# Every fourth low part of the weights: an accumulating DMA onto -hi in place of a subtraction on VectorE

## The chip, the cores and the metric

The kernel runs on one core of one Trainium2 chip. The metric is device time in microseconds (us) of one execution; lower is better. The engines are called as the profile calls them: PE (TensorE, matrix products), DVE (VectorE), ACT (ScalarE), POOL (GpSimd) and SP (SyncE, which issues most DMAs). hi and lo are the two parts of a number, explained below.

## What is computed

One decoder block over 256 tokens of width 2048 in float32, with two attention branches, gates and a feed-forward part. Cut to its products:

```python
xn = rmsnorm(h, attn_norm)
q_a, k_a, v_a, c_q, c_kv, k_r, gates = split(xn @ w_in)
y_a = moba_attention(rope(q_a), rope(k_a), v_a)              # 8 heads of 128
qh = rmsnorm(c_q, q_norm) @ w_uq;  kv = rmsnorm(c_kv, kv_norm) @ w_ukv
y_b = mla_attention(q_nope, rope(q_rope), k_nope, rope(k_r), v_b)
mixed = g_a * (y_a @ w_branch_a) + g_b * (y_b @ w_branch_b)
h = h + mixed @ w_out
hn = rmsnorm(h, ffn_norm)
h = h + (silu(hn @ w_gate) * (hn @ w_up)) @ w_down           # d_ff = 5632
out = rmsnorm(h, final_norm)
```

Both attentions are causal over the 256 tokens. Most of the work is the products with the large weights (about 62 million numbers, each read once).

## The kernel before

Each matrix product is made of float32r passes. An operand is cut into hi (its rounding to float32r) and lo = operand - hi, and hi*hi + lo*hi + hi*lo is summed in PSUM. The activations are stationary (128 rows of the contraction by 128 tokens, two token tiles); the weights stream past them in slabs of 128 rows by 512 columns.

A list of products (`job`) is cut into groups of up to four slabs and into steps of two slabs. There are 468 steps of weights. From the first gate product of the feed-forward part on (`ga0`, step 204) they are 11 pairs of products with w_gate and w_up (176 steps) and 4 products with w_down (88 steps). The last six steps run for one token tile and then for the other.

Work that surrounds one step s:

- `load(g)` (line 722) issues on SP the DMA of one group of weights, 128 x 4 x 512 numbers (1024 KB), into one of four raw tiles. It is called from `split` at the last step of a group, for the group four further on, and has to wait until that raw tile has been read.
- `split(s)` (line 731) makes the pair of weight tiles `wh`, `wl` (two slabs, 128 x 1024 numbers, 512 KB each) from the raw tile: ACT casts hi (line 742), DVE subtracts (line 743). The pool `splitp` has four buffers of each kind (AHEAD + 1), and `split` runs three steps ahead of the products (line 792).
- The products of step s (lines 802 to 810): for each of the two slabs and two token tiles a matmul of wh with the activation's hi, then of wh with its lo (line 805), then of wl with hi (line 810). Twelve matmuls in all. Between the steps stand the small works of attention, transposes and norms, put there by `later` and `at`.

So the wh buffer of step s is free after the eighth matmul of the step, the wl buffer after the twelfth, and both are next used by step s + 4. Every engine works through its instructions in order. The order is the one in which the program issues them (a manual schedule); waits between engines are semaphores. POOL has only a handful of fills at the start.

The lines that the change touches:

```python
nc.scalar.copy(hi, v)
nc.vector.tensor_sub(lo, v, f32(hi))
splits[s] = (hi, lo)
if st["end"]:
    del raws[st["g"]]
    load(st["g"] + RAWS)
```

Of the kernel before, what the change touches and what calls it, by code (L numbers as in the profile page):

```python
"""Hybrid decoder block (MoBA + MLA branches, sigmoid gates, SwiGLU FFN) on one core.

Every matrix product runs in float32r passes: an operand is cut exactly into hi (the float32r
rounding of it) and lo = operand - hi, and hi*hi + lo*hi + hi*lo is summed in float32 in PSUM.
Activations are stationary (transposed, [K, tokens]); weights stream through as [K, 512] slabs.
RMSNorm: gains are applied per partition while the transposed operand leaves PSUM, the
1/rms per token while the product leaves PSUM.
"""
# [2 lines left out]

# [11 lines left out]
OP = mybir.AluOpType  # L23

P = 128
NT = 2
S = NT * P
# [15 lines left out]
START = 8  # L43
# [19 lines left out]
def block_kernel(ctx: ExitStack, tc, x, positions, attn_norm, w_in, q_norm, w_uq, kv_norm, w_ukv,  # L63
                 w_branch_a, w_branch_b, w_out, ffn_norm, w_gate, w_up, w_down, final_norm,
                 inv_freq, out):
    nc = tc.nc
# [8 lines left out]
    def const(shape, name, dt=F32):  # L75
        return consts.tile(shape, dt, name=name)

    def big(shape, name, dt=F32):
        assert int(np.prod(shape[1:])) == 1024
        return tpool.tile(shape, dt, name=name, tag="T")  # L80

    def tps(shape, name):
        return psum.tile(shape, F32, name=name, tag="tp")

    f32 = lambda ap: ap.bitcast(F32)

    # ------------------------------------------------------------------ setup
    grow = [big([P, 1024], f"grow{i}")[:, :P] for i in range(2)]
    for g in grow:
        nc.vector.memset(g, 0.0)  # L90
# [19 lines left out]

    load_gain("attn", attn_norm)

    # mask: [tri | 0 | tri], added to scores [q, k]
    mask = const([P, 3, P], "mask")
    nc.gpsimd.memset(mask, 0.0)
    for j in (0, 2):
# [12 lines left out]
    def gain(key, k):  # L129
        return gT[key != "attn"][:, gcol[key] + k: gcol[key] + k + 1]  # L130

    # ------------------------------------------------------------ small helpers
    def rstd(ss, n, name):
        """ss [P, NT, m] partial sums of squares over n elements -> [P, NT] of 1/rms, in two parts."""
        v, r, t = [const([P, NT], name + x) for x in ("_v", "", "_t")]

        def root():
            nc.vector.tensor_reduce(out=v, in_=ss, axis=mybir.AxisListType.X, op=OP.add)
            nc.vector.tensor_scalar(v, v, 1.0 / n, EPS, op0=OP.mult, op1=OP.add)
            nc.scalar.activation(t, v, AF.Sqrt)  # L140

        def invert():
            nc.vector.reciprocal(r, t)
            nc.vector.tensor_mul(t, r, r)
            nc.vector.tensor_mul(t, t, v)
            nc.vector.tensor_scalar(t, t, -0.5, 1.5, op0=OP.mult, op1=OP.add)
            nc.vector.tensor_mul(r, r, t)
        return r, root, invert
# [4 lines left out]
        nc.scalar.activation(junk[:, :src.shape[-1]], src, AF.Square, accum_out=acc)  # L153

    def split_out(src, hi, lo, scale=None):
        """src -> hi + lo (float32r), scale a [P, 1] factor per partition."""
        if scale is None:
            nc.scalar.copy(hi, src)
            nc.vector.tensor_sub(lo, src, f32(hi))
        else:  # L160
            nc.scalar.mul(hi, src, scale)
            nc.vector.scalar_tensor_tensor(lo, src, scale, f32(hi), op0=OP.mult, op1=OP.subtract)

    def transpose4(nat, hi, lo, name, key=None, k0=0, nk=4, j0=0, first=False):
        """columns j0*128 .. nk*128 of nat [P tok, NT, :] -> hi, lo [P, :, S] at the same j, times the gains."""
        for j in range(j0, nk, 2):
            tp = tps([P, 2, S], f"{name}_tp{j}")
            for k in range(2):
                for t in range(NT):
                    nc.tensor.transpose(tp[:, k, t * P:(t + 1) * P],  # L170
                                        nat[:, t, (j + k) * P:(j + k + 1) * P], ident)
            if key is None:
                split_out(tp, hi[:, j:j + 2, :], lo[:, j:j + 2, :])
            else:
                gk = [gain(key, k0 + j + k) for k in range(2)]
                for k in range(2):
                    if first:
                        nc.vector.tensor_scalar(hi[:, j + k, :], tp[:, k, :], gk[k], None, op0=OP.mult)
                    else:
                        nc.scalar.mul(hi[:, j + k, :], tp[:, k, :], gk[k])  # L180
                for k in range(2):
                    nc.vector.scalar_tensor_tensor(lo[:, j + k, :], tp[:, k, :], gk[k], f32(hi[:, j + k, :]),
                                                   op0=OP.mult, op1=OP.subtract)
# [11 lines left out]
        nc.vector.tensor_sub(o1, ts[0], ts[1])  # L195
        nc.vector.tensor_add(o2, ts[2], ts[3])

    # ------------------------------------------------------------ rope tables
    rt = {}

    def rope_tables():
        """The parts, to be issued in this order. Angle / 2pi is summed from exact products of
        12-bit parts of the angle and of 1 / 2pi, whole turns taken off each."""
        v = nc.vector
        sh = [P, NT, 32]
        c = _inv2pi_parts()
# [1 line left out]
        a, ah, al = const(sh, "ang"), const(sh, "angh", F32R), const(sh, "angl")  # L208
# [50 lines left out]

        return [angles, products, sums, wrap, fold, sines]  # L260

    # ------------------------------------------------------------ streams
    jobs = []

    def job(w, kt, lhs, done, name):
        jobs.append(dict(w=w, kt=kt, n=w.shape[1], lhs=lhs, done=done, name=name))
# [8 lines left out]
        return lambda kt, t: (tiles_hi[kt // 4][:, kt % 4, t * P:(t + 1) * P],  # L275
                              tiles_lo[kt // 4][:, kt % 4, t * P:(t + 1) * P])

    # ------------------------------------------------------------ phase 1: x -> xT, projections
    ssx = const([P, NT, 4], "ssx")
    xh = [big([P, 4, S], f"xh{c}", F32R) for c in range(4)]  # L280
    xl = [big([P, 4, S], f"xl{c}", F32R) for c in range(4)]
# [20 lines left out]
    L = {}  # L302

    R["x"], x_root, x_invert = rstd(ssx, D, "rstd_x")
    ssq, sskv = const([P, NT, 1], "ss_q"), const([P, NT, 1], "ss_kv")
    R["q"], q_root, q_invert = rstd(ssq, QR, "rstd_q")
    R["kv"], kv_root, kv_invert = rstd(sskv, KVR, "rstd_kv")

# [45 lines left out]
    gates = {}  # L354
# [8 lines left out]
        g = gates[key, c]  # L363
        nc.scalar.activation(g, g, AF.Sigmoid)

    # ------------------------------------------------------------ attention
    yT = {}
    PT = [const([P, 2, 512], f"PT{i}", F32R) for i in range(2)]
    for p in PT:
        nc.gpsimd.memset(f32(p[:, :, 0:P]), 0.0)  # L370

    def attention(branch, h, passes, v_of, scale, d1=3, d2=2):
        """passes(t) -> [(lhsT, rhs)] for the scores of query tile t: for t = 0 against the hi and the
        lo parts of the first 128 keys side by side (to be added), for t = 1 against all 256 keys."""
        st = {}

        def stage_s():
# [45 lines left out]
        stage_s()  # L423

    def scores(t, lh, ll, k):
        """k [P, 2 (hi, lo), S]"""
        if t == 0:
            return [(l, k[:, :, 0:P]) for l in (lh, ll)]
        return [(lh, k[:, 0]), (lh, k[:, 1]), (ll, k[:, 0])]
# [2 lines left out]
        yT[b] = ([big([P, 4, S], f"y{b}h{i}", F32R) for i in range(2)],  # L432
                 [big([P, 4, S], f"y{b}l{i}", F32R) for i in range(2)])

    # MLA head pairs
    def uq_done(c):
        def done(ps):
            nat = big([P, NT, 512], f"qn{c}")
# [70 lines left out]
        attention("b", 2 * c + j, passes,  # L509
                  lambda kt: (v[:, 0, kt, j * P:(j + 1) * P], v[:, 1, kt, j * P:(j + 1) * P]), SC_B)  # L510

    # MoBA: SEQ == MOBA_BLOCK, so every query's own block is block 0 and no past block exists
    def qk_done(key, c):
        def done(ps):
            nat = big([P, NT, 512], f"{key}a{c}")
# [39 lines left out]
        attention("a", 4 * c + j, passes,  # L555
                  lambda kt: (vh[:, kt, j * P:(j + 1) * P], vl[:, kt, j * P:(j + 1) * P]), SC_A)

    # ------------------------------------------------------------ branches, merge, FFN
    def wb_done(c):
        def done(ps):  # L560
            g = gates["b", c]
            for t in range(NT):
                nc.vector.tensor_mul(g[:, t], ps[t], g[:, t])
        return done
# [93 lines left out]
                nc.scalar.mul(hc, hc, r)  # L658
            nc.sync.dma_start(o_dram[:, t, c * 512:(c + 1) * 512], hc)

    # ------------------------------------------------------------ the list of products
    job(win(CQ0, QR), 16, xlhs, cq_done, "cq")

    def gate_job(key, c):
# [32 lines left out]
    for c in range(4):  # L697
        job(w_down[:, 512 * c:512 * (c + 1)], 44, lhs_of(ah, al_), down_done(c), f"dn{c}")

    # ------------------------------------------------------------ issue  # L700
    groups, steps = [], []
    for jb in jobs:
        jb["step0"] = len(steps)
        k0 = 0
        while k0 < jb["kt"]:
            nk = min(2 if len(groups) < 2 else 4, jb["kt"] - k0)
# [2 lines left out]
            for k in range(k0, k0 + nk, 2):  # L709
                steps.append(dict(job=jb, k0=k, g=gi, off=k - k0, end=k + 2 >= k0 + nk, toks=(0, 1), src=len(steps)))  # L710
            k0 += nk
    # the last steps run for one token tile, then for the other, so that the first leaves early
    tail = steps[-TAIL:]
    steps[-TAIL:] = [dict(st, toks=(t,)) for t in range(NT) for st in tail]
    step_of = {jb["name"]: jb["step0"] for jb in jobs}
# [15 lines left out]
    def split(s):  # L731
        if s >= len(steps) or steps[s]["src"] != s:
            return
        st = steps[s]
        n = st["job"]["n"]
        v = raws[st["g"]][:, st["off"]:st["off"] + 2, :]
        if len(st["toks"]) < NT:
            hi, lo = big([P, 2, 512], f"wh{s}", F32R), big([P, 2, 512], f"wl{s}", F32R)
        else:
            hi = splitp.tile([P, 2, 512], F32R, name=f"wh{s}", tag="wh")[:, :, :n]  # L740
            lo = splitp.tile([P, 2, 512], F32R, name=f"wl{s}", tag="wl")[:, :, :n]
        nc.scalar.copy(hi, v)  # L742
        nc.vector.tensor_sub(lo, v, f32(hi))  # L743
        splits[s] = (hi, lo)
        if st["end"]:
            del raws[st["g"]]
            load(st["g"] + RAWS)
# [27 lines left out]
    angles, products, sums, wrap, fold, sines = rope_tables()  # L775
# [13 lines left out]
    for s, st in enumerate(steps):  # L789
# [7 lines left out]
        jb, k0, n = st["job"], st["k0"], st["job"]["n"]  # L797
        if k0 == 0:
            accs = [psum.tile([P, 512], F32, name=f"acc{s}_{t}", tag="acc")[:, :n] for t in range(NT)]
        hi, lo = splits[st["src"]]  # L800
        last = k0 + 2 >= jb["kt"]
# [39 lines left out]
```

## Time and profile before

| | us |
|---|---|
| median of two timed runs | 1344.84 (1344.64 to 1345.04) |
| span of the profiled execution, first to last instruction | 1342.6 |
| PE busy | 1327.8 (99%) |
| DVE busy | 742.2 (55%) |
| ACT busy | 629.8 (47%) |
| POOL busy | 2.1 |
| DMA engines busy, mean of 16 | 57% |

Besides its span no time of its own is given for the profiled execution; the median of the timed runs lies 2.2 us above the span. The busy time of an engine is the sum over its instructions. It tells how much work there is, not where an engine is waited for; for that one looks at stretches, at the chain of work that ended last and at the timeline. Matmuls overlap in the records (one shows 0.39 us, and four in a row 1.07 us), so a row of four tells more than one alone. A DMA's time to landing is from its issue to the moment at which its data have arrived.

### The profile page before, as it was taken

To read this page: it belongs to the slowest core of one execution; us is meant where nothing else is said; L and a number is where in the kernel's file an instruction comes from. 1 tells how busy PE (TensorE), PEld (TensorE's weight loads), DVE (VectorE), ACT (ScalarE), POOL (GpSimd) and SP (SyncE) were. 2 spreads that over 40 slices of the span, in tenths; PEclk is the share of its full clock that TensorE was granted. 3 is DMA by queue.
4 is the path that set the end of the run, shared out by engine and by line. 5 is a ranking of instruction groups with operands and counts; after the bars stand their busy time and mean duration, and the time that the engine had idled before them with its cause. 6 is when DMAs were issued, how large, how long until landed. Compare 5 with 4: busy or idle time off the path is not lost.

```text
span 1342.6 us, 15600 instructions
## 1 busy us (share of the span) xinstructions
PE 1327.8 (99%) x6146; PEld 1107.6 (82%) x6146; DVE 742.2 (55%) x1017; ACT 629.8 (47%) x807; POOL 2.1 (0%) x11
## 2 busy tenths in 40 slices
PE   8999999999999999999999999999999999999997
PEld 6888888888888888888888888888888888888885
DVE  5766667574565566555554445444544454545453
ACT  6455555654444454546344444444444443434352
POOL 0000000000000000000000000000000000000000
PEclk9999999999999999999999999999999999999999
DMA  8565454455555555555565556656555565555551
GB/s 295 184 207 185 165 156 152 158 180 189 188 179 166 188 188 188 188 184 187 188 193 189 188 188 188 188 188 188 189 188 188 188 219 191 197 199 197 188 188 63
DMA packets 126966, 249.04 MB, mean 185 GB/s; under 512 B 4486, under 2 KB 9132, under 8 KB 126892
## 3 DMA queue, kind: packets, MB, share of 16 engines
q1 hardware_dynamic: 126620, 247.78, 56.7%
q8 instruction: 48, 0.79, 0.2%
q10 hardware_dynamic: 272, 0.26, 0.1%
q14 instruction: 26, 0.21, 0.1%
HBM read 245.93 MB, written 2.10 MB: 185 GB/s over the span
## 4 chain that ended last, share of the span: by engine, by line
PE 99%; DMA 0%; ACT 0%; DVE 0%; SPq 0%; ACTq 0%; issue 0%
PE acc L805 63%; PE acc L810 31%; PE aT_tp L170 1%; PE sb L382 1%; PE yb L418 0%; PE ya L418 0%; DMA x<-in_x_dram 0%; PE sa L382 0%; PE xT_tp L170 0%; PE mT_tp L170 0%; PE hT_tp L170 0%; PE pTa L405 0%; PE pTb L405 0%; PE kT_tp L170 0%; PE qn_tp L462 0%; PE qT_tp L170 0%
## 5 line engine op out<-in xcount | busy, mean ns | idle before, releaser
L743 DVE TENSOR_TENSOR wl<-raw,wh 128x1024 fp32r<-128x1024 f32 (+2 forms) x468 | 564.4, 1213 | 515.8 <-ACT wh L742 466.8
L742 ACT CAST wh<-raw 128x1024 fp32r<-128x1024 f32 (+2 forms) x468 | 486.2, 1043 | 547.5 <-PE acc L805 525.0
L805 PE MATMUL acc<-wh,hh 128*128 128x512 f32 x704 | 190.5, 392 | 0.0
L805 PE MATMUL acc<-wh,hl 128*128 128x512 f32 x704 | 188.4, 389 | 0.0
L810 PE MATMUL acc<-wl,hh 128*128 128x512 f32 x704 | 188.3, 389 | 0.0
L805 PEld LDWEIGHTS acc<-wh,hl 128*128 128x128 f32 x704 | 132.2, 188 | 27.9
L810 PEld LDWEIGHTS acc<-wl,hh 128*128 128x128 f32 x704 | 132.2, 188 | 27.6
L805 PEld LDWEIGHTS acc<-wh,hh 128*128 128x128 f32 x704 | 130.5, 188 | 25.9
L805 PE MATMUL acc<-wh,xh 128*128 128x512 f32 (+1 forms) x512 | 139.4, 394 | 0.0
L805 PE MATMUL acc<-wh,xl 128*128 128x512 f32 (+1 forms) x512 | 135.6, 387 | 0.0
L810 PE MATMUL acc<-wl,xh 128*128 128x512 f32 (+1 forms) x512 | 135.0, 386 | 0.0
L805 PEld LDWEIGHTS acc<-wh,xl 128*128 128x128 f32 x512 | 95.7, 189 | 19.8
L810 PEld LDWEIGHTS acc<-wl,xh 128*128 128x128 f32 x512 | 95.6, 189 | 19.4
L805 PEld LDWEIGHTS acc<-wh,xh 128*128 128x128 f32 x512 | 91.8, 189 | 15.2
L805 PE MATMUL acc<-wh,ah 128*128 128x512 f32 x352 | 95.3, 390 | 0.0
L805 PE MATMUL acc<-wh,al 128*128 128x512 f32 x352 | 95.1, 389 | 0.0
L810 PE MATMUL acc<-wl,ah 128*128 128x512 f32 x352 | 95.1, 389 | 0.0
L805 PEld LDWEIGHTS acc<-wh,al 128*128 128x128 f32 x352 | 66.1, 188 | 13.8
L810 PEld LDWEIGHTS acc<-wl,ah 128*128 128x128 f32 x352 | 66.1, 188 | 13.7
L805 PEld LDWEIGHTS acc<-wh,ah 128*128 128x128 f32 x352 | 65.9, 188 | 13.6
L153 ACT ACTIVATE junk<-x 128x512 bf16<-128x512 f32 (+1 forms) x26 | 15.5, 598 | 42.6 <-DVE x L643 18.1
L805 PE MATMUL acc<-wh,mh 128*128 128x512 f32 x128 | 35.1, 396 | 0.0
(262 smaller groups left out, 896.7 us busy)
## 6 DMA issues: line engine op xcount, KB each, us to landing
raw<-in_w_in_dram SPq DMA_DIRECT2D x59, 1024.0 KB, 5.1
raw<-in_w_gate_dram SPq DMA_DIRECT2D x44, 1024.0 KB, 5.2
raw<-in_w_up_dram SPq DMA_DIRECT2D x44, 1024.0 KB, 5.2
raw<-in_w_down_dram SPq DMA_DIRECT2D x44, 1024.0 KB, 5.1
raw<-in_w_out_dram SPq DMA_DIRECT2D x16, 1024.0 KB, 5.2
raw<-in_w_branch_b_dram SPq DMA_DIRECT2D x8, 1024.0 KB, 5.1
raw<-in_w_branch_a_dram SPq DMA_DIRECT2D x8, 1024.0 KB, 5.1
raw<-in_w_uq_dram SPq DMA_DIRECT2D x4, 768.0 KB, 4.6
```

The costliest lines, as they stand in the source:

```text
L153: nc.scalar.activation(junk[:, :src.shape[-1]], src, AF.Square, accum_out=acc)
L170: nc.tensor.transpose(tp[:, k, t * P:(t + 1) * P], nat[:, t, (j + k) * P:(j + k + 1) * P], ident)
L382: nc.tensor.matmul(ps[:, t, :], lhsT=l, rhs=r, start=i == 0, stop=i == len(mm) - 1)
L742: nc.scalar.copy(hi, v)
L743: nc.vector.tensor_sub(lo, v, f32(hi))
L805: nc.tensor.matmul(accs[t], lhsT=jb["lhs"](k0 + k, t)[i], rhs=hi[:, k], start=i == 0 and k0 + k == 0, stop=False)
L810: nc.tensor.matmul(accs[t], lhsT=lh, rhs=lo[:, k], start=False, stop=last and k == 1)
```

## The change

From step 8 on, in each step s with s % 4 = 3 (without the last six), lo is not made by DVE. ACT writes -hi into lo (it multiplies the raw tile by -1 and rounds to float32r), and a DMA issued on POOL adds the weights to it, in place. Where s % 8 = 3 the source of the DMA is the raw tile; where s % 8 = 7 it is the weights in DRAM, which are read a second time. All other steps are as before. The comments and descriptions that the diff also takes out are left away here.

```diff
         nc.scalar.copy(hi, v)
-        nc.vector.tensor_sub(lo, v, f32(hi))
+        if s >= START and s % 4 == 3 and len(st["toks"]) == NT:
+
+            nc.scalar.mul(lo, v, -1.0)
+            src = v
+            if s % 8 == 7:
+                jb = st["job"]
+                src = jb["w"][st["k0"] * P:(st["k0"] + 2) * P, :].rearrange("(k p) n -> p k n", p=P)
+            nc.gpsimd.dma_start(lo if s % 8 == 7 else f32(lo), src, accum_op=OP.add)
+        else:
+            nc.vector.tensor_sub(lo, v, f32(hi))
         splits[s] = (hi, lo)
```

In the program of ACT this puts one more instruction behind every fourth cast. Before, in the feed-forward part around the steps 258 and 259 (a row is the line, the operation, output<-inputs with the tile's number, the shape, and what it waits for; the last two figures of a name are those of the allocation):

```order
L742 CAST wh_6050<-raw_5914 128x1024 [waits DMAHW7_49,DVE_49,PE_49]
L742 CAST wh_6066<-raw_5914 128x1024 [waits DVE_49,PE_49]
L742 CAST wh_6084<-raw_5948 128x1024 [waits DMAHW0_49,DVE_49,PE_49]
L742 CAST wh_6100<-raw_5948 128x1024 [waits DVE_49,PE_49]
L742 CAST wh_6118<-raw_5986 128x1024 [waits DMAHW1_49,DVE_49,PE_49]
```

and in the changed kernel at the same place:

```order
L742 CAST wh_6112<-raw_5975 128x1024 [waits DMAHW7_49,DVE_49,PE_49]
L742 CAST wh_6128<-raw_5975 128x1024 [waits PE_49,Activation_49]
L745 ACTIVATE wl_6129<-raw_5975 128x1024 [waits DMASW5_49,PE_49]
L742 CAST wh_6147<-raw_6009 128x1024 [waits DMAHW0_49,DVE_49,PE_49]
L742 CAST wh_6163<-raw_6009 128x1024 [waits DVE_49,PE_49]
L742 CAST wh_6181<-raw_6048 128x1024 [waits DMAHW1_49,DVE_49,PE_49]
```

The multiplication (L745) for step 259 stands between the casts of the steps 259 and 260 and waits for PE's last read of the buffer of wl (and for an earlier DMA of POOL, marked DMASW, into it).

In POOL's program, where nothing stood in the feed-forward part, there are now these, one for every fourth step, in turn from a raw tile and from DRAM:

```order
L750 DMA wl_5971<-raw_5832 128x1024 [waits DMAHW3_49,DMASW3_49,Activation_49]
L750 DMA wl_6044<-in_w_gate_dram 128x2x512 [waits DMASW4_49,Activation_49]
L750 DMA wl_6129<-raw_5975 128x1024 [waits DMAHW7_49,DMASW5_49,Activation_49]
L750 DMA wl_6201<-in_w_up_dram 128x2x512 [waits DMASW6_49,PE_49,Activation_49]
L750 DMA wl_6272<-raw_6133 128x1024 [waits DMAHW3_49,DMASW7_49,Activation_49]
```

Each waits for ACT's multiplication. In SP's program the load that refills a raw tile from which such a DMA reads now waits for that DMA (DMASW6 in the first row), and the load two further on, behind a step with the source in DRAM, for ACT in addition to DVE:

```order
L728 DMA raw152_6735<-in_w_up_dram 128x4x512 [waits DMASW6_49,DMAHW7_49,DVE_49,Activation_49]
L728 DMA raw153_6769<-in_w_gate_dram 128x4x512 [waits DMAHW0_49,DVE_49]
L728 DMA raw154_6807<-in_w_gate_dram 128x4x512 [waits DMAHW1_49,DVE_49,Activation_49]
L728 DMA raw155_6843<-in_w_gate_dram 128x4x512 [waits DMAHW2_49,DVE_49]
L728 DMA raw156_6878<-in_w_gate_dram 128x4x512 [waits DMASW0_49,DMAHW3_49,DVE_49,Activation_49]
```

PE's program has the same matmuls in the same order; the first matmul on such a wl waits for POOL's DMA in place of DVE.

## Rows read from the trace of the kernel before

**Rows 1.** The page's first part: busy us (share of the span) and instructions.

```profile
span 1342.6 us, 15600 instructions
PE 1327.8 (99%) x6146; PEld 1107.6 (82%) x6146; DVE 742.2 (55%) x1017; ACT 629.8 (47%) x807; POOL 2.1 (0%) x11
```

**Rows 2.** Busy time by stretches: stretch, its length, then the engines' busy us.

```profile
core 0: us, PE busy (x) PEld busy (x) DVE busy (x) ACT busy (x) POOL busy (x), PEclk, DMA share, GB/s
0.00:40.00 40.00, 34.09 (x153) 27.93 (x154) 23.64 (x38) 25.63 (x47) 2.11 (x11) 1.00 0.85 285
...
620.00:1000.00 380.00, 380.00 (x1708) 314.55 (x1707) 186.88 (x170) 165.53 (x172) 0.00 (x0) 1.00 0.60 190
1000.00:1300.00 300.00, 300.00 (x1337) 248.41 (x1335) 149.08 (x136) 125.68 (x133) 0.00 (x0) 1.00 0.58 195
1300.00:1342.00 42.00, 33.71 (x149) 27.60 (x147) 16.24 (x27) 13.98 (x23) 0.00 (x0) 0.94 0.25 90
```

**Rows 3.** The chain that ended last, by engine, and its first long piece of matmuls.

```profile
PE 99%; DMA 0%; ACT 0%; DVE 0%; SPq 0%; ACTq 0%; issue 0%
...
8.32 3.41 PE acc L805 x8
```

**Rows 4.** Timeline of a plain stretch: start, length, engine, line, operation [idle before <-releaser].

```profile
900.97 1.05 ACT L742 CAST wh<-raw 128x1024 fp32r<-128x1024 f32 x1 [1.67 <-PE acc L805]
...
902.58 1.07 PE L805 MATMUL acc<-wh,hl 128*128 128x512 f32 x4
...
903.49 1.07 PE L810 MATMUL acc<-wl,hh 128*128 128x512 f32 x4
903.69 1.05 ACT L742 CAST wh<-raw 128x1024 fp32r<-128x1024 f32 x1 [1.67 <-PE acc L805]
...
904.77 1.23 DVE L743 TENSOR_TENSOR wl<-raw,wh 128x1024 fp32r<-128x1024 f32 x1 [1.49 <-ACT wh L742]
...
906.41 1.05 ACT L742 CAST wh<-raw 128x1024 fp32r<-128x1024 f32 x1 [1.67 <-PE acc L805]
...
909.83 1.07 PE L805 MATMUL acc<-wh,hh 128*128 128x512 f32 x4
```

**Rows 5.** The page's costliest groups, DVE's: busy us, mean ns | idle before.

```profile
L743 DVE TENSOR_TENSOR wl<-raw,wh 128x1024 fp32r<-128x1024 f32 (+2 forms) x468 | 564.4, 1213 | 515.8 <-ACT wh L742 466.8
```

**Rows 6.** Instructions on wl, by operand: ns min/median/max, first and last start.

```profile
L810 PE MATMUL acc<-wl,hh x704: 389/389/395, 605.7 to 1093.0; 128*128 128x512 f32 x176
```

**Rows 7.** DMA issues: output<-input, queue, count, KB each, median us to landing.

```profile
raw<-in_w_in_dram SPq DMA_DIRECT2D x59, 1024.0 KB, 5.1
raw<-in_w_gate_dram SPq DMA_DIRECT2D x44, 1024.0 KB, 5.2
...
raw<-in_w_ukv_dram SPq DMA_DIRECT2D x4, 512.0 KB, 3.7
...
x<-in_x_dram SPq DMA_DIRECT2D x3, 512.0 KB, 10.4
...
gf<-in_final_norm_dram SPq DMA_DIRECT2D x2, 512.0 KB, 6.9
```

**Rows 8.** Short stretches: two of one load each, and the loads of gf.

```profile
904.04:909.48 5.44, 5.44 (x26) 4.50 (x25) 2.45 (x2) 2.11 (x3) 0.00 (x0) 1.00 0.60 198
909.48:914.92 5.44, 5.44 (x26) 4.50 (x25) 2.45 (x2) 2.11 (x3) 0.00 (x0) 1.00 0.60 186
...
1096.00:1104.00 8.00, 8.00 (x41) 6.67 (x40) 4.88 (x5) 3.57 (x5) 0.00 (x0) 1.00 0.91 312
```

**Rows 9.** Timeline of SP's issues about gf: start, length, line, issue.

```profile
1089.41 6.49 SPq L728 DMA_DIRECT2D raw<-in_w_down_dram  x2
1095.95 0.98 SPq L618 DMA_DIRECT2D gf<-in_final_norm_dram  x2
```

**Rows 10.** Waits of SP's queue: us in total, times, longest.

```profile
SPq L728 <- DVE wl L743: 1022.1, 201, 8.9
```

## The prediction

> **What bounds the kernel now.** I read the busy times first: TensorE (PE) is busy for 99% of the span, VectorE (DVE) for 55%, ScalarE (ACT) for 47%, and GpSimd (POOL) for 2.1 us in all [rows 1]. Then the stretches, because a mean hides where an engine stands still: from 620 to 1300 us PE is busy for the whole of each stretch at a granted clock of 1.00, and of the 14.8 us of the span in which PE is idle (1342.6 - 1327.8), 40.0 - 34.1 = 5.9 lie before 40 us and 42.0 - 33.7 = 8.3 after 1300, so at the two ends [rows 2]. The chain that ended last says the same: PE 99%, nearly all of it on lines 805 and 810 [rows 3]. So DVE's time, from which the change takes, is on no path that sets the end. What can change the end is only a wait of PE.
>
> Next, what lies between PE and a new pair of weight tiles. The timeline of a plain stretch shows a pattern that repeats every 2.72 us (the ACT casts start at 900.97, 903.69, 906.41 [rows 4]): a step of PE is four matmuls on wh with the activation's hi, four on wh with its lo, four on wl with hi. The cast of a later step starts 0.04 us after PE ends its last read of wh, so it waits for the buffer and not for ACT. There are four buffers of each kind; the tile made then is read by PE four steps later, 4 x 2.72 = 10.88 us.
>
> **The change part by part.** It touches the steps s = 11, 15, ... 459: 113 of 468, of which 57 take the source from the raw tile and 56 (s = 15, 23, ... 455) read the weights again from DRAM.
>
> Removed: 113 subtractions of about 1.21 us on DVE [rows 5], 137 us, 742 to 605. Worth nothing, since PE does not wait for it.
>
> Added on ACT: 113 multiplications by -1 over the same 128x1024 tile as the cast, which takes 1.05 us [rows 4]: 119 us, 630 to 749, 56% of the span. Hidden in the 1.67 us for which ACT is idle before each cast. Example: the cast at 903.69 ends at 904.74; PE's last read of the wl buffer to be refilled ends at 903.49 + 1.07 = 904.56; the multiplication can run from 904.75 to 905.8, and the next cast is due at 906.41. Where a silu or another cast stands between, the next cast slips by some tenths, and it has time: it ends at 902.02 in the pattern and its first matmul comes at 909.83, 7.8 us later. Cost nothing; if that cover were gone, at most 113 x 1.05 = 119 us.
>
> Added on POOL and in the DMA engines: 113 accumulating DMAs, each waiting for the multiplication. POOL has nothing else to do, so nothing is queued behind one but the next, 10.88 us later. PE waits for it before the first matmul on wl. That is the step that decides. **The budget**: wl's matmuls of that step started at 903.49 in the example, so four steps later they start at 914.37; from 905.8 this leaves 8.57 us, 8.5 after the two hand-overs of 0.03 to 0.04 us. The same in a ring: the wl buffer of these steps is always the same one of the four, and PE's read (1.07), the multiplication (1.05) and the DMA must go round it in 10.88 us. In the 204 steps ahead of the first gate product PE also has attention and projections: they take from 8.3 [rows 3] to 603.9 us (wl's matmuls on hh, third of the step, start at 605.7 [rows 6]), 2.92 us each, so the budget there is on average 4 x 0.20 = 0.8 us longer, 9.3.
>
> **What the DMA takes** is not in the trace: there is no DMA from POOL and none that adds. From below: a load of as many bytes, 512 KB from w_ukv, lands 3.7 us after its issue [rows 7]. An accumulation has to read its destination as well as its source, 1024 KB in all; a load of 1024 KB lands after 5.1 to 5.2 us. Beside other traffic: the two 512 KB loads of gf were issued one behind the other at 1096, right after a weight load [rows 9], and landed after 6.9 us, in a stretch with the DMA engines busy at 0.91 [rows 7, 8]. From above: the 512 KB loads of x at the start, in a queue of loads, took 10.4 us [rows 7]. Which applies: for the raw source, the load that refills the raw slot now waits on SP for the accumulation itself, so the accumulation runs in the gap after the load before, which is issued 5.44 us earlier and has landed; I take 5.2 us. For the DRAM source the next load is issued about when the accumulation is, since ACT and no longer DVE is the last to read that raw tile; I take gf's 6.9 us. Both are under 8.5, by 3.3 and 1.6 us, and this margin also has to hold what POOL needs to issue a DMA, which no row shows.
>
> The two reads are also what the Trainium skill states ("Collectives: The Full Stack", Part 3): the adding transfer reads two sources for one write and runs at half the rate of a copy. No run here shows it yet.
>
> **What else the DMA touches.** A 1024 KB load takes 0.60 x 5.44 = 3.3 us of the DMA engines [rows 8]; two loads per 10.88 us make 6.5, and an accumulation that costs as much as a load makes 9.8, 0.90 of the time. Tight, but 0.91 was held at 1096 to 1104 us without an idle PE [rows 8]. The refill of a raw slot slips from DVE's end (about 906.0) to the landing, about 911 in the example. SP issues in order, so the load behind it may slip as well. The raw tile is first wanted seven steps after its slot's last cast, 903.69 + 19.04 = 922.7; issued at 911.0 and landed 5.2 us later it is there at 916.2, so 6.5 us remain. SP's waits for DVE [rows 10] are such early waits and cost nothing.
>
> **Sum.** 1342.6 us of span - 0 + 0 + 0, and the 2.2 us by which the median of the timed runs (1344.84) exceeds the span: 1344.8, which I round to **1345 us**; its own range is 1341 to 1352.
>
> **The rivals.**
> 1. *Only the DRAM half is late.* These run beside a weight load. If the two share the engines evenly and the accumulation lands after 10.4 us like the x loads, PE stands still 1.9 us in the 32 cases after 603.9 us and 1.1 us in the 24 before: 61 + 26 = 87 us, **1432 us**. It decides from 8.5 us on and costs 2% (27 us) from about 9.0. For it: 0.90 busy engines and a second read. Against: gf's 6.9 us.
> 2. *Every accumulation is late*, because adding or issuing from POOL is slower than any load here. At 10.4 us for all: 64 x 1.9 + 49 x 1.1 = 176 us, **1520 us**, and each further us adds 113. For it: no row bounds POOL's part. Against: 3.3 us of margin for the raw half. A slower PE also gives its cycle more room, so it does not run away.
> 3. *POOL is held while DVE works.* If POOL could not prepare its DMA while a subtraction runs, and lost two of them, 2 x 1.23 us [rows 4], the DRAM half would land after 6.9 + 2.5 = 9.4 us, 0.9 late after 603.9 us and 0.1 before: 32 x 0.9 + 24 x 0.1 = 31 us, **1376 us**. The raw half (7.7) stays in time. For it: in a plain step DVE is busy 1.23 of 2.72 us. Against: one DMA has three steps in which to find DVE idle.
> The Trainium skill ("SBUF — State Buffer", "Who interferes with whom") speaks for this rival in general: DVE and GpSimd share a pair of ports and a DMA issued from GpSimd can wait for DVE. It excepts the two-input subtraction, which is nearly all that DVE does here, and by that the sum stays 1345. No row of before tests it.
> 4. *Faster by over 2%.* It would need PE's idle time, 14.8 us in all, which is 1.1%, and lies at the ends, where the change adds nothing. A different matmul time is not in the change.
>
> **Chances.** Hidden 0.56, rival 1 0.17, rival 2 0.18, rival 3 0.07, faster 0.02. Runs of this kernel tell about 2% from no change: faster 0.02, same 0.56, slower 0.42. The range leaves out rival 2 with most of its mass above 1480 (0.16) and a little below 1340 (0.02): **1340 to 1480**.
>
> **What would show it.** In the profile after: PE still 99% busy and no idle time ahead of line 819 on wl from POOL's DMA; DVE near 605 and ACT near 749 us; 113 DMAs from POOL with a landing of 5 to 7 us, the DRAM half longer; DMA share up from about 57% to between 70 and 84%. I am wrong if their landing is over 8.5 us. Idle time of PE at every eighth step is rival 1, at every fourth rival 2; a landing that varies with DVE's subtractions is rival 3. A granted clock below 1.00 in the middle would mean that the waits cost more than their length.

## The result and the profile after

The changed kernel takes 1400.3 us (1398.6 to 1402.1) where the kernel before takes 1344.8: slower by 4.15%, 95% interval 3.82 to 4.48%, 55.5 us. The profiled execution has a span of 1400.3 us against 1342.6, 57.7 more.

The page's first part, which answers to [rows 1] (busy us, share of the span, instructions):

```profile
span 1400.3 us, 15893 instructions
PE 1342.4 (96%) x6146; PEld 1107.8 (79%) x6146; DVE 612.0 (44%) x904; ACT 736.0 (53%) x920; POOL 121.9 (9%) x124
```

DVE lost 130 us of work, ACT gained 106 and POOL 120. None of that shows in the time. PE executes the same 6146 matmuls and stands idle for 1400.3 - 1342.4 = 57.9 us in place of 14.8. Where, the instructions on wl tell. From the list of who waited for the tile wl (us, times):

```profile
  PEld acc L819: 57.2, 37
  PE acc L819: 42.1, 30
```

PEld is the load of the stationary operand; its wait and that of the matmul behind it are one wait, seen twice, and a part of it still counts as busy, because the matmuls before are being finished. Before the change nothing of PE waited here. PEld runs a little ahead of PE, so its 57.2 us are somewhat more than PE lost. PE executes the same matmuls in the same order in both traces; set side by side start by start, 47.7 of the 57.7 us come in front of the first matmul on such a wl. Of the other 10 about 5 belong to the clock (below), and the rest is scattered in small pieces. By the source of POOL's DMA, PEld's waits are (largest first):

```profile
PEld acc L819 <- DMA wl<-in_w_up_dram: 22.6, 11, 3.1
...
PEld acc L819 <- DMA wl<-in_w_down_dram: 11.7, 10, 2.7
PEld acc L819 <- DMA wl<-in_w_in_dram: 10.8, 6, 3.4
...
PEld acc L819 <- DMA wl<-in_w_out_dram: 6.7, 4, 2.1
```

Behind accumulations from the raw tile there is a single wait, of 0.5 us; all others have DRAM as source. The time from issue to landing says why. The list of DMA issues (count, KB each, median us to landing):

```profile
wl<-raw POOLq DMA_DIRECT2D x55, 512.0 KB, 4.6
...
wl<-in_w_in_dram POOLq DMA_DIRECT2D x14, 512.0 KB, 8.2
wl<-in_w_gate_dram POOLq DMA_DIRECT2D x11, 512.0 KB, 8.2
wl<-in_w_up_dram POOLq DMA_DIRECT2D x11, 512.0 KB, 8.3
wl<-in_w_down_dram POOLq DMA_DIRECT2D x10, 512.0 KB, 8.8
```

Two kinds, 4.6 and 8.2 to 8.8 us in these four groups (the eight from w_out and the branches lie at 8.5 to 9.3). One of the late ones in the timeline (start, length, engine, line, operation, [idle before <-releaser]), an accumulation from w_up:

```profile
970.03 1.07 PE L819 MATMUL acc<-wl,hh 128*128 128x512 f32 x4
970.69 1.27 ACT L602 ACTIVATE sil<-acc,rstd_h 128x512 f32<-128x512 f32 x2 [2.12 <-PE acc L819]
...
971.84 1.05 ACT L742 CAST wh<-raw 128x1024 fp32r<-128x1024 f32 x1
...
972.78 1.07 ACT L745 ACTIVATE wl<-raw 128x1024 fp32r<-128x1024 f32 x1
...
974.27 1.21 POOL L750 DMA_DIRECT2D wl<-in_w_up_dram  x1 [11.60 <-ACT wl L745]
...
983.15 1.20 PE L819 MATMUL acc<-wl,hh 128*128 128x512 f32 x4 [2.08 <-DMA wl<-in_w_up_dram]
```

The wl buffer is free at 970.03 + 1.07 = 971.1. The multiplication starts at 972.78, 1.7 us later, because two silu activations and the cast stand ahead of it in ACT's queue. It ends at 973.85; POOL starts 0.42 us later, and the sum lands 8.8 us after that, at 983.1. PE would have been there at 970.03 + 10.88 = 980.9.

What those 8.8 us contain is seen in the DMA queues over two neighbouring stretches. From 974.2 to 978.2 us, then from 978.2 to 982.6 (queue: packets, MB, share of the 16 engines; q1 is SP's, q0 is POOL's):

```profile
q1 hardware_dynamic: 431, 0.88, 78.7%
```

```profile
q0 software_dynamic: 271, 0.52, 68.0%
q1 hardware_dynamic: 314, 0.61, 37.3%
```

For 3.9 us after its issue POOL's queue moves nothing. SP's refill load, which ACT's multiplication released too and which was issued 0.4 us before (973.87), goes first. Only then do the 512 KB of the accumulation move, 4.4 x 0.68 = 3.0 us of all engines. An accumulation from the raw tile, issued at 961.77, in busy time by stretches (stretch, length, five engines' busy us, PE's granted clock, share of the DMA engines, GB/s):

```profile
961.70:963.20 1.50, 1.50 (x8) 1.26 (x7) 0.04 (x1) 1.05 (x1) 0.91 (x1) 1.00 0.00 0
963.20:966.20 3.00, 3.00 (x15) 2.46 (x14) 1.51 (x2) 1.05 (x1) 0.00 (x0) 1.00 0.92 175
```

It starts to move data 1.5 us after its issue, with the engines to itself, and is through in another 3: its refill waits for it. Two accumulations from w_in show the same for DRAM as source in this very kernel: at 111.2 and 186.2 us SP's refill was held up and issued 3.0 and 2.1 us after POOL's DMA, and they landed after 6.2 and 5.9 us, with the first data about 2 us after the issue.

A smaller loss comes on top. After three of PE's waits the granted clock fell for a short time: right after the one shown, which was 2.08 us, and after waits of 2.63 and 2.29 us that ended at 1078.5 and 1151.5 us. After other waits of that length it did not fall (3.14 us, ended at 74.3; 2.04 us, ended at 1289.7). The stretch after the first (the third number from the end is the granted clock as a share of 2.4 GHz; 0.51 is 1.2 GHz for nearly all of it):

```profile
984.20:987.60 3.40, 3.40 (x10) 2.63 (x9) 0.00 (x0) 1.06 (x1) 0.90 (x1) 0.51 0.16 37
```

Three such stretches of 3.4 us at half the clock are 3 x 1.7 = 5 us of PE's work. In the kernel before the clock is 1.00 in the stretches from 620 to 1300 us [rows 2].

### The profile page after: what moved, and what is told of

The parts are those of the page before. It is cut to its first block, busy times and chain, and to the rows that moved or that the text cites. A ratio compares the mean times of both kernels' runs of the same rounds, so it can differ in the third digit from the quotient of the medians.

```text
span 1400.3 us, 15893 instructions
## 1 busy us (share of the span) xinstructions
PE 1342.4 (96%) x6146; PEld 1107.8 (79%) x6146; DVE 612.0 (44%) x904; ACT 736.0 (53%) x920; POOL 121.9 (9%) x124
## 3 DMA queue, kind: packets, MB, share of 16 engines
q0 software_dynamic: 23696, 58.60, 23.2%
## 5 line engine op out<-in xcount | busy, mean ns | idle before, releaser
L752 DVE TENSOR_TENSOR wl<-raw,wh 128x1024 fp32r<-128x1024 f32 (+1 forms) x355 | 429.9, 1214 | 672.1 <-ACT wh L742 651.5
L819 PEld LDWEIGHTS acc<-wl,hh 128*128 128x128 f32 x704 | 131.8, 189 | 52.3 <-DMA wl<-in_w_up_dram 22.6
L745 ACT ACTIVATE wl<-raw 128x1024 fp32r<-128x1024 f32 (+2 forms) x113 | 118.7, 1050 | 41.9 <-PE acc L819 41.7
L750 POOL DMA_DIRECT2D wl<-raw x57 | 51.8, 909 | 626.2 <-ACT wl L745 499.8
```

The source lines that it names most:

```text
L745: nc.scalar.mul(lo, v, -1.0)
L750: nc.gpsimd.dma_start(lo if s % 8 == 7 else f32(lo), src, accum_op=OP.add)
L819: nc.tensor.matmul(accs[t], lhsT=lh, rhs=lo[:, k], start=False, stop=last and k == 1)
```

## The experiments

The theory after the result: **queue**. An accumulation from DRAM is late because it stands behind the refill load that is issued at the same moment; one from the raw tile holds its refill back and has the engines to itself. Its rivals: **source** (reading DRAM while adding is slow in itself), **amount** (the DMA engines, 0.76 busy in place of 0.57, slow everything) and, for a part of the loss, **ACT's queue** (the silu ahead of the multiplication). The table gathers the results; the last column is the wait of PEld for POOL's DMAs in the profiled execution. Each ratio is against the kernel before on the same chip.

| kernel | us | ratio (95%) | PEld waits, us |
|---|---|---|---|
| changed | 1400.3 | 1.0415 (1.0382 to 1.0448) | 57.2 |
| raw half only | 1345.2 | 1.0007 (0.9998 to 1.0017) | 0.5 |
| DRAM half only | 1396.0 | 1.0384 (1.0368 to 1.0399) | 50.3 |
| all from the raw tile | 1356.2 | 1.0090 (1.0065 to 1.0115) | 10.7 |
| refill held in the DRAM half | 1379.4 | 1.0265 (1.0244 to 1.0285) | 41.2 |
| DRAM half one step earlier | 1362.1 | 1.0133 (1.0115 to 1.0151) | 21.1 |
| DRAM half only, one step earlier | 1348.5 | 1.0026 (1.0016 to 1.0035) | 3.4 |
| accumulations onto a scratch tile | 1344.8 | 1.0003 (0.9993 to 1.0012) | none |
| -hi made on DVE | 1380.4 | 1.0282 (1.0246 to 1.0318) | 35.6 |
| copies in place of sums | 1350.5 | 1.0046 (1.0028 to 1.0064) | 4.9 |

In every row the loss and the wait of PEld agree within some 6 us.

**One half alone.**

```diff
-        if s >= START and s % 4 == 3 and len(st["toks"]) == NT:
+        if s >= START and s % 8 == 3 and len(st["toks"]) == NT:
```

and for the other half `s % 8 == 7`.

> Only the accumulations with the raw tile as source are kept (s % 8 = 3, 57 of 113); where the source was DRAM, DVE subtracts again. Queue theory (an accumulation from DRAM is late because it stands behind the refill load that is issued at the same moment; one from the raw tile makes its refill wait and has the engines for itself): landing 4.6 us as in the changed kernel, under the 8.5 us that PE leaves, no wait of PE: 1343 to 1350 us. Amount theory (the loss comes from the DMA engines being busy at 0.78 in place of 0.59, whatever the order): half of the added traffic, half of the loss, about 1372 us. Source theory (reading DRAM while adding is slow in itself): 1343 to 1350 us too.

> Only the accumulations with DRAM as source are kept (s % 8 = 7, 56 of 113); where the source was the raw tile, DVE subtracts again. Queue theory: each still meets the refill load of its own raw slot, landing 8 to 9 us, the loss stays nearly whole: 1385 to 1402 us. Source theory: the same. Amount theory: about 1372 us.

The raw half costs nothing that can be measured, and the DRAM half by itself costs 51.7 of the 55.5 us. Amount falls: with half of the traffic the loss is nothing or nearly everything. Queue and source remain.

**All from the raw tile**, and **the refill held back**:

```diff
-            if s % 8 == 7:
+            if False:
...
-            nc.gpsimd.dma_start(lo if s % 8 == 7 else f32(lo), src, accum_op=OP.add)
+            nc.gpsimd.dma_start(f32(lo), src, accum_op=OP.add)
```

```diff
+            if s % 8 == 7:
+                nc.gpsimd.tensor_add(probe, f32(lo)[:, 0, 0:1], v[:, 0, 0:1])
```

> All 113 accumulations take the raw tile as source, so that each refill load waits for its accumulation. Queue theory: landing 4.6 to 5.5 us for all, PE does not wait: 1343 to 1352 us, with the DMA engines about as busy as in the changed kernel (0.75 to 0.8). Source theory: the same. Amount theory: 1390 to 1400 us.

> As the changed kernel, with DRAM as source of every second accumulation; after each of these POOL reads one column of the raw tile and of the sum (128 numbers each), so that the refill load of that raw slot can only start when the accumulation has landed. Queue theory: the DRAM half lands after 5.5 to 6.5 us in place of 8.2 to 8.8, PE waits nearly nowhere: 1343 to 1358 us. Source theory: the landing stays above 8 us and the time at 1390 to 1402 us. Amount theory: 1390 to 1402 us.

Both missed their numbers, and the misses decide between source and queue. With the refill held, the landing of the DRAM half fell, but not everywhere, and that of the raw half rose (list of DMA issues, held refill):

```profile
wl<-raw POOLq DMA_DIRECT2D x55, 512.0 KB, 8.3
...
wl<-in_w_in_dram POOLq DMA_DIRECT2D x14, 512.0 KB, 5.7
wl<-in_w_gate_dram POOLq DMA_DIRECT2D x11, 512.0 KB, 7.9
wl<-in_w_up_dram POOLq DMA_DIRECT2D x11, 512.0 KB, 6.1
wl<-in_w_down_dram POOLq DMA_DIRECT2D x10, 512.0 KB, 8.4
```

So do the waits: most of them now stand behind the raw half (PEld, us, times, longest):

```profile
PEld acc L822 <- DMA wl<-raw: 30.7, 32, 2.6
```

The same accumulation from the raw tile takes 4.6 us in the changed kernel and 8.3 here. The held refill and the next one, which waits behind it on SP, now run when the raw half is issued (in the example SP issues both from 944.71 us on, and the accumulation follows at 947.47). In the 4.7 us after the issue of one of these (947.4 to 952.1 us) the queues show SP alone:

```profile
q1 hardware_dynamic: 786, 1.58, 98.0%
```

So an accumulation from the raw tile is as late as one from DRAM when loads stand ahead of it, and one from DRAM lands after 5.7 to 6.1 us where the loads were issued earlier. Source falls. With all from the raw tile the refills are held as well, and the landing rises to 5.2 us in the median and up to 9.6: 10.7 us of waits are left.

**The moment.** If queue is right, it is enough to move the accumulations from DRAM by one step, to where no refill starts:

```diff
-        if s >= START and s % 4 == 3 and len(st["toks"]) == NT:
+        if s >= START and s % 8 in (3, 6) and len(st["toks"]) == NT:
...
-            if s % 8 == 7:
+            if s % 8 == 6:
```

> The accumulations from DRAM are moved by one step, from s % 8 = 7 to s % 8 = 6, the first step of its group, which starts no refill; those from the raw tile stay at s % 8 = 3. Traffic, sources and the number of accumulations are the same. Queue theory: the load refilled after the step before was issued about 2.9 us earlier and is nearly through when the accumulation's data could start, so the DRAM half lands after about 6 us (1.8 to the first data, 3.5 of data, 0.7 to the landing): PE does not wait, 1343 to 1355 us. Amount theory: nothing changes, 1392 to 1402 us.

It gained 38 of the 55 us and missed its range by 7: the landing was 6.7 to 7.1 us for w_in, w_gate and w_up, 8.8 for w_down. A guess at the rest was that the refills held by the raw half still came in between. Without the raw half:

```diff
-        if s >= START and s % 8 in (3, 6) and len(st["toks"]) == NT:
+        if s >= START and s % 8 == 6 and len(st["toks"]) == NT:
```

> Only accumulations from DRAM, 58 of them, at s % 8 = 6; DVE subtracts in all other steps, so that no refill is held back by an accumulation from the raw tile. It differs from the kernel with the DRAM half alone (1396 us) by one step in time only. Queue theory, with the addition that the held refills of the raw half brought the loads behind the moved accumulations in the kernel before this one: the refill of the odd step before is nearly through, landing about 6 us for all sources, 1343 to 1350 us. If the DRAM half is late wherever it stands: 1385 to 1400 us; if half of the remaining 18 us belong to it without the raw half: about 1353 us.

(There are 56 accumulations by the profile, not 58.) The list of DMA issues of this kernel:

```profile
wl<-in_w_in_dram POOLq DMA_DIRECT2D x14, 512.0 KB, 5.8
wl<-in_w_gate_dram POOLq DMA_DIRECT2D x11, 512.0 KB, 5.9
wl<-in_w_up_dram POOLq DMA_DIRECT2D x11, 512.0 KB, 5.9
wl<-in_w_down_dram POOLq DMA_DIRECT2D x10, 512.0 KB, 6.1
```

The DRAM half alone costs 51.7 us at one step and 3.7 us one step earlier, with the same bytes from the same place. The landing went from about 8.4 to 5.9 us for all sources; that shows queue. Not all of the 48 us are proof of it: one step earlier, the multiplication for w_up also stands ahead of the silu (it starts 0.1 us after its buffer is free, and 1.7 us after in the kernel with the DRAM half at s % 8 = 7).

**The wait and not the traffic.** The sums onto a tile that nobody reads, beside the subtractions on DVE (a scratch tile of [P, 2, 512] and 32 large tiles in place of 33):

```diff
         nc.vector.tensor_sub(lo, v, f32(hi))
+        if s >= START and s % 4 == 3 and len(st["toks"]) == NT:
...
+            nc.scalar.mul(scratch[:, :, :n], v, -1.0)
+            nc.gpsimd.dma_start(scratch[:, :, :n], src, accum_op=OP.add)
```

> DVE makes every lo as before the change; beside it ACT's multiplication and POOL's accumulations run at the same steps and from the same sources, onto a scratch tile that no product reads (one buffer less in the pool of large tiles for its space). Queue theory: the DRAM half lands as late as in the changed kernel, about 8.3 us, but PE waits for none of them: 1343 to 1348 us. Amount theory (the traffic itself holds the loads or PE back): 1375 to 1400 us.

As expected: 1.0003, with landings from DRAM of 7.8 to 9.9 us. So the traffic, ACT's extra work and the later refills cost nothing as long as PE does not wait for the sums.

**ACT's queue.**

```diff
-            nc.scalar.mul(lo, v, -1.0)
+            nc.vector.tensor_scalar(lo, v, -1.0, None, op0=OP.mult)
```

> As the changed kernel, but DVE and not ACT writes -hi. That takes the delay in ACT's queue away, where the multiplication stands behind two silu activations (2 x 0.64 us) and a cast that waited for them. If this delay is a part of the loss, as the trace of the changed kernel suggests for the 11 accumulations from w_up (about 1.7 us each): 19 us less, about 1381 us, and PE's wait for them falls from about 2.0 to under 0.5 us each. If the queue of the DMA alone makes the loss: 1396 to 1402 us.

1380.4 us, 19.9 less than the changed kernel. The landing from w_up did not get shorter (8.9 us), but PE's wait for it fell from 22.6 us to

```profile
PEld acc L819 <- DMA wl<-in_w_up_dram: 8.0, 11, 1.8
```

0.73 us each, somewhat more than the 0.5 expected. So 14.6 of the 21.6 us by which PEld's waits fell in all are those behind the silu. Not all of that is ACT's queue: DVE's multiplication is also shorter, 0.69 us in place of 1.06, and at other steps DVE has work of its own ahead of it (0.8 to 2.1 us for w_out).

The trace of the changed kernel shows that the silu is not the only thing in the way. In 22 of the 56 steps with DRAM as source the multiplication starts 1.7 to 2.6 us after its buffer is free: 11 behind the silu, 11 behind the squares for a norm or work on earlier products; in the others it starts within 0.5 us. The landing is the same in both groups (8.3 us in the median), but PE loses more than 0.15 us in 19 of the 22 and in 13 of the 34, and the 22 have 32 of the 47.7 us.

**The second read.**

```diff
-            nc.gpsimd.dma_start(lo if s % 8 == 7 else f32(lo), src, accum_op=OP.add)
+            nc.gpsimd.dma_start(lo if s % 8 == 7 else f32(lo), src)
```

> As the changed kernel, but POOL's DMAs copy the weights into lo and do not add (the sums are therefore not made and lo is the whole weight). It shows the price of the second read: if an accumulation moves its data at half the rate of a copy, the data take about 1.5 us in place of 2.8 to 3.6, the DRAM half lands after about 7 us in place of 8.3, and the loss shrinks from 55 to some 15 to 30 us: 1358 to 1376 us. If adding costs nothing beyond a copy: 1396 to 1402 us.

It came out below the range, 1350.5. The landing fell from 4.6 to 2.9 us for the raw half and from 8.2 to 6.0 for w_in. The queue's line on the page of this kernel, and then of the changed one:

```profile
q0 software_dynamic: 23344, 58.60, 12.2%
```

```profile
q0 software_dynamic: 23696, 58.60, 23.2%
```

For the same 58.6 MB 12.2% of 1349 us against 23.2% of 1400: a sum costs the engines 1.97 times as much as a copy. The landing fell by more than the 1.3 us expected, 2.2 from DRAM. Half a microsecond of that is POOL's instruction, 0.70 us for a copy from DRAM in place of 1.21; the rest stays open.

The copies stand behind the same refills and behind the same work of ACT, and still 49 of the 55 us are gone. So the parts of the loss can't be added up: the loss is what goes over the slack of the ring, and all links share that slack. Without the load ahead 48 of 52 us go (in part by ACT's queue, as said), without the sum 49 of 55, with -hi on DVE 20 of 55.

## Why the prediction was right or wrong

The forecast was 1345 us with 0.56 on no change, and that did not come. The range up to 1480 holds the 1400 only because it was drawn around the rivals. What happened is rival 1, which had 0.17 and 1432 us, by another mechanism than its even share of the DMA engines.

*What held.* DVE's time was worth nothing: 612 us of work were forecast as 605, and no part of the 130 us came back. PE's wait ahead of the products on wl decides, and the ring around that buffer is the budget. The raw half lands after 4.6 us (5.2 forecast) and is hidden, 1.0007. The DMA share of 0.76 lies in the forecast 0.70 to 0.84, and, as said, it does no harm alone (the scratch tile). All waits but one fall on the steps with s % 8 = 7. The last sign came as well: a clock below 1.00 in the middle, so that some waits cost more than their length.

*What failed, first: the landing of the DRAM half.* I took gf's 6.9 us, for two 512 KB loads beside a weight load; it is 8.2 to 9.3. The row was for loads issued on the same queue as the weight load and with one read. The right sum from the rows of after: 1.9 us from the issue to the first data when the way is free (at 186.2 us; 1.21 of it POOL's instruction), about 2.3 standing behind the refill (in the example the first data come 4.2 us after the issue), 3 to 3.7 for the data, 0.3 to the landing. I had seen that the refill is issued at the same moment, and let the two share the engines. That gave 10.4 us for the worst case and 6.9 for the likely one; in truth the load goes first. 8.2 to 8.8 is right at the budget of 8.5, so a plain step mostly loses little or nothing (gate: 2 waits in 11), and a small error in either decides.

*Second: ACT's multiplication "cost nothing".* I looked at what its delay does to the cast behind it, which has 7.8 us to spare, and not at what stands ahead of the multiplication itself, which is in the ring and takes its time from the DMA's budget: 1.7 to 2.6 us in 22 of the 56 steps, 11 of them the silu for w_up. With a landing of 8.3 us nothing was left for that; with one of 6 (the copies) it cost next to nothing. The run with -hi on DVE gave 20 us back.

*Third, a small term:* the hand-over from ACT to POOL, taken as 0.03 to 0.04 us from the hand-overs between the other engines, is 0.31 to 0.43 us (the multiplication ends at 973.85, POOL starts at 974.27).

*The other rivals.* Rival 1's price of 87 us was taken at a landing of 10.4 us in all 56 cases; it was 51.7 in the run with this half alone. Rival 2 did not come: the raw half is in time. Rival 3 did not come either: POOL's instruction takes 1.20 to 1.23 us for every source in DRAM, whatever DVE does (list of the instructions on wl, min/median/max ns),

```profile
L750 POOL DMA_DIRECT2D wl<-in_w_gate_dram x11: 1203/1213/1229, 626.2 to 1093.8; - x11
```

and with 73 us more work on DVE, in the run with -hi on DVE, the landings from DRAM are 8.1 to 9.2 us as against 8.2 to 9.3. The exception that the Trainium skill makes for two-input subtractions ("SBUF — State Buffer", "Who interferes with whom") is borne out here: a subtraction on DVE began at 974.81, within POOL's instruction of 974.27, and that took its usual 1.21 us.

*The weighed page.* The half rate that the Trainium skill states for an adding transfer ("Collectives: The Full Stack", Part 3) agrees with the traces: a sum took 1.97 times the engine time of a copy.

## What to carry to other kernels

When work is moved off a busy engine that nobody waits for, the gain is nothing and the question is only what the new path adds to the ring around each buffer: sum it link by link (the read that frees the buffer, what stands ahead in the queue of each engine on the way, the hand-overs, the issue, the landing), and take for each the worst neighbour and not the plain one. Look for what else is released by the same event: a DMA that starts together with a large load has to be priced as standing behind that load. If it must be there, put it at a step that releases no load; here one step made 52 us into 4. And don't expect the links to have fixed prices: the loss is what exceeds the slack, so shortening one link can remove nearly all of it.

## What the runs showed of the hardware

- POOL's queue and SP's did not share the DMA engines evenly: with loads issued 0.4 to 3 us before it the accumulation moved nothing for 3.9 us (SP's queue had 79% of the engines) and for 4.7 us (98%), where 1.5 us (raw tile) and 1.9 us (DRAM) pass when the way is free. The Trainium skill ("DMA: Bandwidth & Descriptors", "Queues, rings and completion order") states that an engine goes round the queues that have work, packet by packet. Later stretches do show both queues at once (68 and 37%); at the start of a transfer the measurement does not look like that, unless POOL's queue had no work there yet. What sets the order, the moment of issue or something in how POOL's descriptors are fetched, these runs leave open.
- An accumulating DMA of 512 KB from POOL, with the way free: 0.9 us (raw tile, 144 packets in the queue's row) or 1.21 us (DRAM, 271 packets) of POOL's time, first data 1.5 or 1.9 us after the issue, 4.6 or 5.9 us to the landing; the data of one from the raw tile alone take 2.8 us.
- Three waits of PE, of 2.08, 2.63 and 2.29 us, were each followed by 3.4 us at 1.2 GHz, and others of 2.04 and 3.14 us were not. Before the change the granted clock is 1.00 in every stretch up to 1300 us.
